# A feed-forward block product with seven half products in place of eight, its weight sums made on GpSimd

## The chip, the cores and the metric

One core of a Trainium2 chip. The metric is the device time of one execution in microseconds, the median of three runs.

## The reference, cut to what matters

Two layers, each a feed-forward half step, a mixer and a second feed-forward half step, on 256 tokens of width 1024, all in fp32:

```python
D_MODEL = 1024; SEQ = 256; DEPTH = 2; D_FF = 2816
def swiglu_ffn(h, w_up, w_down):
    gate, up = jnp.split(h @ w_up, 2, axis=-1)
    return (jax.nn.silu(gate) * up) @ w_down
...
    for l in range(DEPTH):
        x = x + 0.5 * swiglu_ffn(rms_norm(x, g_ffn1[l]), w_up1[l], w_down1[l])
        ...  # the mixer: recurrence and attention, not touched here
        x = x + 0.5 * swiglu_ffn(rms_norm(x, g_ffn2[l]), w_up2[l], w_down2[l])
```

## The kernel before

Every fp32 product is made of three products of rounded parts: an operand is split into a high part (rounded, type float32r) and a low part (what is left), and high x high, high x low and low x high are added in PSUM. The activations are split once per norm. The weights are split tile by tile as they stream in: a tile (`hc`, 512 KB: two blocks of 128 rows by 512 columns, or one by 1024) is loaded by SP into `raw` (`emit_dma`, five buffers), rounded by ACT into `whi` (`emit_hi`, L331, six buffers), and DVE subtracts to get `wlo` (`emit_lo`, L340, six buffers). TensorE then visits the tile once for each of the two token tiles of 128 (`visit`, L390): two blocks of rows, three matmuls each, so 6 matmuls a visit and 12 a tile. The high part of a tile can be made once the tile six places earlier has had both its visits.

A feed-forward (`ffn`, L603) goes through the hidden width in six chunks (`CH`: five of 512 columns, one of 256). For each chunk `block` makes gate for both token tiles (4 weight tiles), then up (4 tiles). ACT takes the gate out of PSUM through silu into `nat` (`ev_g`, L637), DVE multiplies with up (`ev_u`, L642), and a chain (`h_chain`) transposes that h: a copy into `tmp`, a transposing DMA issued by SP, a copy back by ACT or DVE (L318, L315), and a split into high and low parts (L502, L504). The down product of the chunk before follows each chunk but the first (`down`, 4 tiles).

The order on every engine is written out when the program is built: a planner (`Sched`) keeps a clock per engine, bills each instruction a cost, and lets chains of small work step in between matmuls when their time has come. `split` decides when the next `whi` and `wlo` are placed. The engines then run their queues strictly in this order and wait on semaphores.

POOL does little: constants at the start, the power for the norms (L551), powers for the attention's norms (L950), and its own DMA queue: 22 small loads of parameter rows (`load_rows`, L467 to L472) near the start, and four stores of a tensor of ones to DRAM (`ones_chain`, L681) that ACT prepares with copies (L677). Twelve large buffers (`slot`) hold activations, hidden chunks and scratch in turn.

## Time and profile before

| | us |
|---|---|
| median of 3 runs (1269.89 to 1270.96) | 1269.91 |
| the profiled execution, its own time | 1269.92 |
| its span in the profile | 1268.2 |
| TensorE busy | 1257.6 |
| DVE busy | 825.4 |
| ACT busy | 804.8 |
| POOL busy | 69.5 |

The time of a run and the span of its profile differ by 1.7 us, which lie outside the first and last instruction. Busy times of different engines overlap; a time is the sum of what ended last at each point, which for nearly all of this kernel is TensorE.

### The profile page before, as it was taken

The page shows a single profiled execution, that of the slowest core. Times are in us where ns is not written, and L with a number is a line of the kernel's source. Part 1 is how long each engine was busy: PE and PEld are TensorE (multiplying, and loading weights), DVE is VectorE, ACT ScalarE, POOL GpSimd, SP SyncE. Part 2 cuts the span into 40 slices and gives each one's busy share as a digit, 9 for nine tenths or more (in the row PEclk, how much of TensorE's full clock was granted, in tenths as well). Part 3 has the DMA queues.
Part 4 walks back from the last instruction along what each step waited for, and adds up shares of the span by engine and source line. Part 5 has one row for each costly group of instructions (what it writes and reads, how often), then busy time and mean ns, then how long its engine had stood idle before and what let it go on. Part 6 is the DMA issues. An engine that isn't in the chain of part 4 may idle for free.

```text
span 1268.2 us, 16349 instructions
## 1 busy us (share of the span) xinstructions
PE 1257.6 (99%) x5961; PEld 1039.6 (82%) x5961; DVE 825.4 (65%) x1164; ACT 804.8 (63%) x1076; POOL 69.5 (5%) x89
## 2 busy tenths in 40 slices
PE   9999999999999999999999999999999999999998
PEld 7888888888777888888888888888887878888887
DVE  6655558798676666555575545678977767655553
ACT  6657557886767556555566555679757764665553
POOL 4000000002200000000000000000042000000000
PEclk9999999999999999999999999999999999999999
DMA  7967769676444568676678777597764345687762
GB/s 258 264 207 225 217 172 277 161 218 202 148 141 150 168 198 217 209 208 207 179 220 217 213 216 216 158 249 190 210 206 149 126 150 182 193 222 216 216 199 76
DMA packets 193489, 248.80 MB, mean 196 GB/s; under 512 B 73672, under 2 KB 86144, under 8 KB 193408
## 3 DMA queue, kind: packets, MB, share of 16 engines
q1 hardware_dynamic: 191472, 244.49, 64.8%
q0 software_dynamic: 1920, 3.26, 1.0%
q8 instruction: 47, 0.77, 0.2%
q14 instruction: 34, 0.28, 0.1%
q10 hardware_dynamic: 16, 0.00, 0.0%
HBM read 229.88 MB, written 2.10 MB: 183 GB/s over the span
## 4 chain that ended last, share of the span: by engine, by line
PE 94%; DVE 3%; ACT 1%; DMA 1%; issue 1%; SPq 0%; POOL 0%; ACTq 0%; DVEq 0%
PE x L397 14%; PE x L399 13%; PE x L398 13%; PE z L398 12%; PE z L397 12%; PE z L399 12%; PE y L397 4%; PE y L399 4%; PE y L398 4%; PE z L481 2%; PE z L1008 1%; PE z L818 1%; DVE wlo L340 1%; PE y L1070 1%; DMA raw<-in_w_up_dram 1%
## 5 line engine op out<-in xcount | busy, mean ns | idle before, releaser
L340 DVE TENSOR_TENSOR wlo<-raw,whi 128x1024 fp32r<-128x1024 f32 x423 | 510.3, 1221 | 218.8 <-ACT whi L331 211.4
L331 ACT CAST whi<-raw 128x1024 fp32r<-128x1024 f32 x423 | 440.3, 1049 | 209.2 <-PE z L399 118.0
L397 PE MATMUL x<-whi,s 128*128 128x512 f32 x800 | 322.4, 403 | 4.8 <-DVE nat L954 2.8
L399 PE MATMUL x<-whi,s 128*128 128x512 f32 x800 | 312.5, 391 | 0.0
L398 PE MATMUL x<-wlo,s 128*128 128x512 f32 x800 | 312.2, 390 | 0.0
L398 PE MATMUL z<-wlo,s 128*128 128x512 f32 (+1 forms) x752 | 279.5, 372 | 0.1
L397 PE MATMUL z<-whi,s 128*128 128x512 f32 (+1 forms) x752 | 279.3, 371 | 0.0
L399 PE MATMUL z<-whi,s 128*128 128x512 f32 (+1 forms) x752 | 279.1, 371 | 0.0
L397 PEld LDWEIGHTS x<-whi,s 128*128 128x128 f32 x800 | 150.3, 188 | 38.8 <-issue 2.9
L399 PEld LDWEIGHTS x<-whi,s 128*128 128x128 f32 x800 | 150.2, 188 | 33.3 <-DVE s L504 0.9
L398 PEld LDWEIGHTS x<-wlo,s 128*128 128x128 f32 x800 | 150.5, 188 | 29.4 <-DVE wlo L340 0.6
L398 PEld LDWEIGHTS z<-wlo,s 128*128 128x128 f32 x752 | 141.7, 188 | 25.9 <-DVE wlo L340 1.8
L397 PEld LDWEIGHTS z<-whi,s 128*128 128x128 f32 x752 | 141.7, 188 | 24.4
L399 PEld LDWEIGHTS z<-whi,s 128*128 128x128 f32 x752 | 141.7, 188 | 24.4
L318 ACT COPY tmp<-nat 128x1024 uint16<-128x1024 uint16 (+1 forms) x88 | 96.3, 1114 | 76.2 <-DMA nat<-tmp 68.2
L397 PE MATMUL y<-whi,s 128*128 128x512 f32 x208 | 82.3, 396 | 0.0
L399 PE MATMUL y<-whi,s 128*128 128x512 f32 x208 | 81.1, 390 | 0.0
L398 PE MATMUL y<-wlo,s 128*128 128x512 f32 x208 | 81.0, 390 | 0.0
L642 DVE SCALAR_TENSOR_TENSOR nat<-z,rstd,nat 128x512 f32<-128x512 f32 (+1 forms) x48 | 33.9, 706 | 57.9 <-PE z L399 57.9
L504 DVE TENSOR_TENSOR s<-tmp,s 128x512 fp32r<-128x512 f32 (+1 forms) x71 | 46.6, 657 | 27.4 <-ACT s L502 26.9
L637 ACT ACTIVATE nat<-z,rstd 128x512 f32<-128x512 f32 (+1 forms) x46 | 30.0, 652 | 47.1 <-PE z L399 47.0
L502 ACT CAST s<-tmp 128x512 fp32r<-128x512 f32 (+1 forms) x71 | 42.0, 592 | 20.6 <-DVE tmp L531 19.8
(161 smaller groups left out, 891.0 us busy)
## 6 DMA issues: line engine op xcount, KB each, us to landing
raw<-in_w_up_dram SPq DMA_DIRECT2D x175, 512.0 KB, 4.6
raw<-in_w_in_dram SPq DMA_DIRECT2D x112, 512.0 KB, 4.4
raw<-in_w_down_dram SPq DMA_DIRECT2D x88, 512.0 KB, 4.4
raw<-in_w_lru_out_dram SPq DMA_DIRECT2D x16, 512.0 KB, 3.8
raw<-in_w_attn_out_dram SPq DMA_DIRECT2D x16, 512.0 KB, 3.8
raw<-in_w_o_dram SPq DMA_DIRECT2D x16, 512.0 KB, 4.3
s<-ones_d POOLq DMA_DIRECT2D x16, 128.0 KB, 4.4
tmp<-in_b_gate_dram SPq DMA_DIRECT2D x8, 256.0 KB, 4.3
```

The costliest lines, as they stand in the source:

```text
L318: nc.scalar.copy(out_, in_)
L331: nc.scalar.copy(hi, raws[i])
L340: nc.vector.tensor_tensor(out=lo, in0=raws.pop(i), in1=f32(hi), op=ALU.subtract)
L397: nc.tensor.matmul(acc, lhsT=lhs(0, k0 + kk)[:, ts], rhs=hi[:, kk, :], start=st, stop=False)
L398: nc.tensor.matmul(acc, lhsT=lhs(0, k0 + kk)[:, ts], rhs=lo[:, kk, :], start=False, stop=False)
L399: nc.tensor.matmul(acc, lhsT=lhs(1, k0 + kk)[:, ts], rhs=hi[:, kk, :], start=False, stop=sp)
L481: nc.tensor.transpose(dst_ps[:, j * P:(j + 1) * P], src[:, j * P:(j + 1) * P], ident)
L502: nc.scalar.copy(hi, t)
L504: nc.vector.tensor_tensor(out=lo, in0=t, in1=f32(hi), op=ALU.subtract)
L637: nc.scalar.activation(s[tok][0], acc, AF.Silu, scale=rs(tok))
L642: nc.vector.scalar_tensor_tensor(out=h, in0=acc, scalar=rs(tok), in1=h, op0=ALU.mult, op1=ALU.mult)
L818: nc.tensor.matmul(ps[:, g, :], lhsT=wax[0][:, g, n, :], rhs=xr[0][:, n, :], start=True, stop=True)
```

## The change

For chunks 2 and 4 of every feed-forward (`SEVEN`), gate and up are made as one product of 2 x 2 blocks. The activations are cut into two token tiles by two halves of the 1024 inputs, the weights into two halves of the inputs (rows 0 to 511 and 512 to 1023) by gate and up columns. With Winograd's form of Strassen's scheme seven products of half the depth give all four results, where the plain form needs eight. Four of the seven weight operands are sums: t3 = 22 - 12, t1 = 12 - 11, t2 = 11 + t3, t4 = 21 - t2, made by POOL in fp32 on the loaded tiles (`sums`, L279 of the new file), and then split into high and low parts as any tile. Four activation operands are sums too; POOL makes them once per feed-forward (`sums_chain`, L721 and L728), and ACT and DVE split them. Each of the seven products has two weight tiles, each visited once: 14 tiles of 6 matmuls in place of 8 tiles of 12. The results come together in four buffers of SBUF (`w`): ACT copies the first product, DVE adds the others out of PSUM with seven sums (L757), and the gating follows as before (L764, L769). The products run in the order 11, t1, t2, 21, t3, 22, t4.

The eight loads of a block go to five slots, in the order 11, 12, 22, 21, and are issued in a row right behind the load ahead of them. The loads of the parameter rows stay where they were in time, and their transposes come 45 us earlier, so that their slot comes free.

```diff
+GPS = 2.3
...
+SEVEN = (2, 4)
...
+    ORDER = ("11", "t1", "t2", "21", "t3", "22", "t4")
...
+        def load(self, name, u, src):
+            if not self.t:
+                for k in ("11", "12", "22", "21", "t3"):
+                    self.t[k] = slot([P, 4, 512])
+            nc.sync.dma_start(out=self.part(name, u), in_=src)
+            if name != "12":
+                raws[self.index(name, u)] = self.part(name, u), 0.0
+            if (name, u) == ("21", 1):
+                self.chain = S.add(self.sums(), S.now + 6.0, "g")
+        def sums(self):
+            def op(name, u, dst, a, b, f):
+                o = self.part(dst, u)
+                nc.gpsimd.tensor_tensor(out=o, in0=self.part(a, u), in1=self.part(b, u), op=f)
+                raws[self.index(name, u)] = o, S.use("g", GPS)
+            for u in range(2):
+                op("t3", u, "t3", "22", "12", ALU.subtract)
+                yield S.t["g"], "g"
+                op("t1", u, "12", "12", "11", ALU.subtract)
+                yield S.t["g"], "g"
+            for name, dst, a, b, f in (("t2", "11", "t3", "11", ALU.add), ("t4", "21", "21", "11", ALU.subtract)):
+                for u in range(2):
+                    while nxt["lo"] <= self.index(dst, u):
+                        yield S.now + 0.5, "g"
+                    op(name, u, dst, a, b, f)
+                    yield S.t["g"], "g"
...
+    def plan_seven(w, f0):
+        st = Seven()
+        sevens.append(st)
+        for name, r0, c0 in (("11", 0, f0), ("12", 0, FF + f0), ("22", 512, FF + f0), ("21", 512, f0)):
+            for u in range(2):
+                r = r0 + 256 * u
+                loads.append((w[r:r + 256, c0:c0 + 512].rearrange("(k p) n -> p k n", p=P), (st, name, u)))
+        for _ in range(14):
+            hcs.append((2, 512))
+            uses.append(1)
 
...
+        raws[i] = t, 0.0
+        while loads and isinstance(loads[0][1], tuple):
+            src, (st, name, u) = loads.pop(0)
+            st.load(name, u, src)
...
-        if can_hi() and nxt["hi"] - nxt["pos"] <= lead and (idle is None or S.busy("a") < idle):
+        if can_hi() and nxt["hi"] - nxt["pos"] <= lead and (
+                idle is None or S.busy("a") < idle) and raws[nxt["hi"]][1] <= max(S.now, S.t["a"]) + 0.05:
...
+        def sums_chain():
+            for tok in range(NT):
+                for hf in range(2):
+                    yield nrm.done[tok, hf]
+            xh, xl = nrm.xT[0][0], nrm.xT[1][0]
+            a, b = slot([P, KD, T]), slot([P, 4, 4, P])
+            for q in range(2):
+                yield S.t["g"], "g"
+                ks = slice(4 * q, 4 * q + 4)
+                nc.gpsimd.tensor_tensor(out=a[0][:, ks], in0=f32(xh[:, ks]), in1=f32(xl[:, ks]), op=ALU.add)
+                S.use("g", GPS)
+            A = lambda tok, q: a[0][:, 4 * q:4 * q + 4, tok * P:(tok + 1) * P]
+            B = lambda i: b[0][:, i]
+            for i, u, v, f in ((0, A(1, 0), A(1, 1), ALU.add), (1, B(0), A(0, 0), ALU.subtract),
+                               (2, A(0, 0), A(1, 0), ALU.subtract), (3, A(0, 1), B(1), ALU.subtract)):
+                yield S.t["g"], "g"
+                nc.gpsimd.tensor_tensor(out=B(i), in0=u, in1=v, op=f)
+                S.use("g", GPS / 2)
+            free(a)
+            sums[0], sums[1] = slot([P, 4, 4, P], F32R), slot([P, 4, 4, P], F32R)
+            yield S.t["g"], "a"
+            for q in range(2):
+                ii = slice(2 * q, 2 * q + 2)
+                yield from split_seg(b[0][:, ii], sums[0][0][:, ii], sums[1][0][:, ii], 1024)
+                yield S.now, "a"
+            free(b)
+        sums_c = S.add(sums_chain(), S.now + 4.0, "g", True)
...
+        def seven(c):
+            st = sevens.pop(0)
+            S.need(sums_c)
+            xh = lambda tok, q: lambda e, k: nrm.xT[e][0][:, 4 * q + k, tok * P:(tok + 1) * P]
+            xs = lambda i: lambda e, k: sums[e][0][:, i, k, :]
+            w = slot([P, 4, 512])
+            s1, u2, u4, c22 = (w[0][:, i] for i in range(4))
+            h, b5 = {}, []
+            def prod(name, lhs_, fin):
+                b, r = zbank()
+                for u in range(2):
+                    visit(st.index(name, u), b, lhs_, 2 * u, None, u == 0, u == 1, (lambda: fin(b, r)) if u else None)
+            def plus(dst, x, y, dep=0.0):
+                nc.vector.tensor_tensor(out=dst, in0=x, in1=y, op=ALU.add)
+                return S.use("d", dve_c(512), dep)
+            def gate(tok, src, dep):
+                nrm.scaled(tok)
+                h[tok] = new_nat()
+                S.func("silu")
+                nc.scalar.activation(h[tok][0], src, AF.Silu, scale=rs(tok))
+                return S.use("a", act_c(512, 1), dep)
+            def up(tok, src, dep):
+                t, rh = h[tok]
+                nc.vector.scalar_tensor_tensor(out=t, in0=src, scalar=rs(tok), in1=t, op0=ALU.mult, op1=ALU.mult)
+                dep = S.use("d", dve_c(512), dep)
+                hch[c, tok] = rh.user = S.add(h_chain(c, tok, t, rh, dep), dep)
+            def after_1(b, r):
+                nc.scalar.copy(s1, b)
+                S.use("a", act_c(512))
+                r.free = True
+            def after_6(b, r):
+                plus(u2, b, s1)
+                r.free = True
+                plus(u4, b5[0], u2)
+            def after_2(b, r):
+                end = plus(s1, b, s1)
+                r.free = True
+                gate(0, s1, end)
+            def after_7(b, r):
+                plus(u2, b, u2)
+                r.free = True
+                plus(c22, b5[0], u2)
+                b5[1].free = True
+            def after_3(b, r):
+                end = plus(u4, b, u4)
+                r.free = True
+                up(0, u4, end)
+            def after_4(b, r):
+                end = plus(u2, b, u2)
+                r.free = True
+                up(1, c22, gate(1, u2, end))
+            prod("11", xh(0, 0), after_1)
+            prod("t1", xs(0), lambda b, r: b5.extend((b, r)))
+            prod("t2", xs(1), after_6)
+            prod("21", xh(0, 1), after_2)
+            prod("t3", xs(2), after_7)
+            prod("22", xs(3), after_3)
+            prod("t4", xh(1, 1), after_4)
+            take(14)
...
-        yield S.now + 70.0, "p"
+        yield S.now + 25.0, "p"
```

What this does to the queues, at three places.

The first is the start of the program. POOL's queue before: the two powers of the first norm, then the loads of the parameter rows into `s0`.

```order
L551 TENSOR_TENSOR rstd_110<-msum_109,mhalf_99 128x1 x2
L467 DMA s0_1_101<-in_g_ffn1_dram 8x128
L467 DMA s0_1_101<-in_g_mix_dram 8x128
L467 DMA s0_1_101<-in_g_ffn2_dram 8x128
L467 DMA s0_1_101<-in_conv_b_dram 8x128
L467 DMA s0_1_101<-in_b_a_dram 8x128
```

And now (`s1` and `s2` are the high and low parts of the activations, `s4` their sum, `s5` the four sums of quarters):

```order
L631 TENSOR_TENSOR rstd_110<-msum_109,mhalf_99 128x1 x2
L721 TENSOR_TENSOR s4_36_277<-s1_9_149,s2_10_150 128x1024 x2
L728 TENSOR_TENSOR s5_37_278<-s4_36_277 128x512
L728 TENSOR_TENSOR s5_37_278<-s5_37_278,s4_36_277 128x512
L728 TENSOR_TENSOR s5_37_278<-s4_36_277 128x512
L547 DMA s0_1_101<-in_g_ffn1_dram 8x128
...
L551 DMA s0_1_101<-in_g_k_dram 1x16x4 x2
L552 DMA bfb_106<-in_b_forget_dram 128x16
L728 TENSOR_TENSOR s5_37_278<-s4_36_277,s5_37_278 128x512
```

Five sums stand between the powers and the 22 loads, and the sixth behind the loads. ACT's queue before, from the last roundings of chunk 0 into chunk 1 (`whi_60` and `whi_63` are tiles 10 and 11, the third and fourth of chunk 1's gate):

```order
L331 CAST whi_48_324<-raw_25_216 128x1024
L331 CAST whi_49_358<-raw_37_285 128x1024
L331 CAST whi_52_367<-raw_43_309 128x1024
L331 CAST whi_60_401<-raw_45_313 128x1024
L331 CAST whi_63_413<-raw_51_362 128x1024
L318 COPY tmp_66_422<-nat_40_300 128x1024
```

And now (`s6` takes the high parts of `s5`; `whi_64` is tile 10):

```order
L404 CAST whi_50_331<-raw_25_216 128x1024
L404 CAST whi_53_368<-raw_39_289 128x1024
L404 CAST whi_56_377<-raw_45_314 128x1024
L582 CAST s6_51_363<-s5_37_278 128x1024 x2
L404 CAST whi_64_414<-raw_47_319 128x1024
L404 CAST whi_67_426<-raw_55_372 128x1024
```

Two casts of `s5` stand ahead of tile 10; the second of them reads what POOL's sixth sum writes.

The second place is the ones, in the first feed-forward's chunk 1. ACT's queue before:

```order
L331 CAST whi_162_918<-raw_149_838 128x1024
L677 COPY s6_165_931<-ident_93 32x1024 x3
L502 CAST s5_119_690<-tmp_155_863 128x4x128
L677 COPY s6_165_931<-ident_93 32x1024
L677 COPY s7_166_942<-ident_93 32x1024 x4
L690 CAST fw_168_951<-tmp_167_949 128x8x16
L331 CAST whi_173_974<-raw_152_851 128x1024
```

And now, ACT and then POOL:

```order
L870 COPY s0_104_604<-ident_93 32x1024 x3
L404 CAST whi_105_611<-raw_79_476 128x1024
L870 COPY s0_104_604<-ident_93 32x1024
L870 COPY s0_106_616<-ident_93 32x1024 x4
L883 CAST fw_108_625<-tmp_107_623 128x8x16
L582 CAST s8_71_449<-tmp_109_627 128x4x128
L404 CAST whi_113_661<-raw_84_511 128x1024
```

```order
L728 TENSOR_TENSOR s5_37_278<-s4_36_277,s5_37_278 128x512
L279 TENSOR_TENSOR s5_89_517<-s11_87_515,s10_86_514 128x1024
L279 TENSOR_TENSOR s10_86_514<-s10_86_514,s9_85_513 128x1024
L279 TENSOR_TENSOR s5_89_517<-s11_87_515,s10_86_514 128x1024
L279 TENSOR_TENSOR s10_86_514<-s10_86_514,s9_85_513 128x1024
L874 DMA ones_d0_111<-s0_104_604 64x1024 x2
L874 DMA ones_d1_112<-s0_106_616 64x1024 x2
```

The copies go into one slot (`s0`) twice, where there were two slots, and the stores out of it stand behind four weight sums.

The third is a block in the middle, chunk 2 of the second layer's first feed-forward. DVE's queue before, in the down product of the chunk before and the gate that follows:

```order
L340 TENSOR_TENSOR wlo_1142_5928<-raw_1122_5830,whi_1137_5910 128x1024
L340 TENSOR_TENSOR wlo_1147_5964<-raw_1125_5838,whi_1146_5956 128x1024
L340 TENSOR_TENSOR wlo_1151_5978<-raw_1132_5880,whi_1149_5968 128x1024
L340 TENSOR_TENSOR wlo_1155_5992<-raw_1134_5888,whi_1150_5976 128x1024
L340 TENSOR_TENSOR wlo_1158_6006<-raw_1141_5922,whi_1154_5990 128x1024
L642 SCALAR_TENSOR_TENSOR nat_1144_5947<-z_1157_5996,rstd_110,nat_1144_5947 128x512
L315 COPY tmp_1162_6035<-nat_1144_5947 128x1024
```

And now, from the first tile of t2 (`s4`) to the fourth sum:

```order
L413 TENSOR_TENSOR wlo_1207_6092<-s4_1164_5877,whi_1201_6070 128x1024
L584 TENSOR_TENSOR s3_1152_5819<-tmp_1193_6016,s3_1152_5819 128x4x128
L413 TENSOR_TENSOR wlo_1208_6098<-s4_1164_5877,whi_1202_6079 128x1024
L413 TENSOR_TENSOR wlo_1211_6110<-s11_1167_5880,whi_1206_6090 128x1024
L413 TENSOR_TENSOR wlo_1213_6118<-s11_1167_5880,whi_1209_6104 128x1024
L413 TENSOR_TENSOR wlo_1215_6129<-s6_1168_5881,whi_1212_6116 128x1024
L413 TENSOR_TENSOR wlo_1218_6140<-s6_1168_5881,whi_1214_6127 128x1024
L757 TENSOR_TENSOR s8_1204_6082<-z_1216_6131,s8_1204_6082 128x512
L757 TENSOR_TENSOR s8_1204_6082<-z_1210_6106,s8_1204_6082 128x512
L413 TENSOR_TENSOR wlo_1222_6161<-s5_1166_5879,whi_1217_6138 128x1024
L413 TENSOR_TENSOR wlo_1223_6166<-s5_1166_5879,whi_1219_6150 128x1024
L757 TENSOR_TENSOR s8_1204_6082<-z_1220_6152,s8_1204_6082 128x512
```

Where a tile's split stood for 12 matmuls it now stands for 6, and the sums out of `z` stand between the splits.

## Rows read from the trace of the kernel before

**Rows 1.** The page: busy us, share of span, instructions; then the chain by engine.

```profile
PE 1257.6 (99%) x5961; PEld 1039.6 (82%) x5961; DVE 825.4 (65%) x1164; ACT 804.8 (63%) x1076; POOL 69.5 (5%) x89
PE 94%; DVE 3%; ACT 1%; DMA 1%; issue 1%; SPq 0%; POOL 0%; ACTq 0%; DVEq 0%
```

**Rows 2.** Windows view: us, PE, PEld, DVE, ACT, POOL busy (instructions), clock, DMA share, GB/s.

```profile
660.00:682.00 22.00, 22.00 (x99) 18.23 (x98) 13.26 (x14) 14.29 (x16) 0.00 (x0) 1.00 0.86 209
```

**Rows 3.** Timeline of PE: start, us, instruction; 24 matmuls lie between these two starts.

```profile
480.43 0.39 PE L397 MATMUL z<-whi,s 128*128 128x512 f32 x1
...
485.87 0.39 PE L397 MATMUL z<-whi,s 128*128 128x512 f32 x1
```

**Rows 4.** The page's groups (count, busy, mean ns), then DVE's timeline in the first 20 us.

```profile
L340 DVE TENSOR_TENSOR wlo<-raw,whi 128x1024 fp32r<-128x1024 f32 x423 | 510.3, 1221 | 218.8 <-ACT whi L331 211.4
L331 ACT CAST whi<-raw 128x1024 fp32r<-128x1024 f32 x423 | 440.3, 1049 | 209.2 <-PE z L399 118.0
13.76 1.28 DVE L531 TENSOR_TENSOR tmp<-z,g1col 128x512 f32<-128x512 f32 x2
17.29 3.50 DVE L340 TENSOR_TENSOR wlo<-raw,whi 128x1024 fp32r<-128x1024 f32 x3 [0.36 <-ACT whi L331]
```

**Rows 5.** Timeline of POOL from the start: all it does before 36 us, in part.

```profile
1.08 0.29 POOL masks.py:199 TENSOR_SCALAR_AFFINE_SELECT ident<-ident 128x128 f32<-128x128 f32 x1
...
1.83 0.31 POOL L1190 MEMSET posm<- 128x256 f32 x1
...
16.23 1.39 POOL L551 TENSOR_TENSOR rstd<-msum,mhalf 128x1 f32<-128x1 f32 x2 [13.06 <-DVE msum L549]
17.57 0.72 POOL L467 DMA_DIRECT2D s<-in_g_ffn_dram  x1
...
34.99 0.59 POOL L472 DMA_DIRECT2D bfb<-in_b_forget_dram  x1
```

**Rows 6.** Timelines of ACT and DVE from 28 to 33 us.

```profile
28.66 1.05 ACT L331 CAST whi<-raw 128x1024 fp32r<-128x1024 f32 x1 [2.24 <-PE z L399]
29.75 2.59 DVE L340 TENSOR_TENSOR wlo<-raw,whi 128x1024 fp32r<-128x1024 f32 x2 [1.03 <-ACT whi L331]
32.81 0.75 DVE L642 SCALAR_TENSOR_TENSOR nat<-z,rstd,nat 128x512 f32<-128x512 f32 x1 [0.48 <-PE z L399]
```

**Rows 7.** ACT, POOL and PE from 99 to 111 us; landing of the stores to ones_d.

```profile
99.05 3.15 ACT L677 COPY s<-ident 32x1024 f32<-32x1024 f32 x3
...
102.88 5.29 ACT L677 COPY s<-ident 32x1024 f32<-32x1024 f32 x5
102.50 0.56 POOL L681 DMA_DIRECT2D ones_d<-s  x1 [66.93 <-ACT s L677]
110.75 0.50 PE L398 MATMUL z<-wlo,s 128*128 128x512 f32 x1
DMA to landing us min/median/max: 2.9/2.9/3.0
```

**Rows 8.** ACT near 692 us; then DMA issues, 645 to 720 us.

```profile
692.17 1.35 ACT L318 COPY tmp<-nat 128x1024 uint16<-128x1024 uint16 x1 [2.98 <-DMA nat<-tmp]
raw<-in_w_up_dram SPq DMA_DIRECT2D x21, 512.0 KB, 4.7
nat<-tmp SPq DMA_TRANSPOSE x6, 4.5
```

**Rows 9.** POOL's powers of 128x8 and DVE's splits beside them, from 304 to 324 us.

```profile
304.86 2.59 POOL L950 TENSOR_TENSOR rq<-rq,mhalf 128x8 f32<-128x8 f32 x1 [4.38 <-DVE rq L948]
311.91 2.57 POOL L950 TENSOR_TENSOR rq<-rq,mhalf 128x8 f32<-128x8 f32 x1 [3.46 <-DVE rq L948]
322.17 1.64 POOL L950 TENSOR_TENSOR rq<-rq,mhalf 128x8 f32<-128x8 f32 x1 [2.60 <-DVE rq L948]
304.72 1.23 DVE L340 TENSOR_TENSOR wlo<-raw,whi 128x1024 fp32r<-128x1024 f32 x1
311.73 3.69 DVE L340 TENSOR_TENSOR wlo<-raw,whi 128x1024 fp32r<-128x1024 f32 x3
```

More of the change, by code (lines that the diff above doesn't have):

```diff
@@ L323, in can_hi @@
         i = nxt["hi"]
-        return i < NHC and i in raws and (i < RING or used[i - RING] == NT)
+        return i < NHC and i in raws and (i < RING or used[i - RING] == uses[i - RING])
     def emit_hi():
@@ L383, in get_hc @@
             if nxt["hi"] == nxt["lo"]:
+                for st in sevens:
+                    if st.i0 <= nxt["hi"] < st.i0 + 14:
+                        while nxt["hi"] not in raws:
+                            S.step(st.chain, True)
                 assert can_hi()
@@ L392, in visit @@
         hi, lo = get_hc(i)
-        _, nk, ncol = hcs[i]
-        ts = slice(tok * P, tok * P + P)
+        nk, ncol = hcs[i]
+        ts = slice(tok * P, tok * P + P) if tok is not None else slice(0, P)
         for kk in range(nk):
@@ L402, in visit @@
                 used[i] += 1
[L403 removed]
+                if used[i] == uses[i]:
                     ready.pop(i)
@@ new lines, in ffn @@
+        sums_c = S.add(sums_chain(), S.now + 4.0, "g", True)
[58 more added lines that the diff above has]
+            take(14)
+            st.release()
+            free(w)
+            if c == SEVEN[-1]:
+                free(sums[0])
+                free(sums[1])
```

60 lines of the change are left out of this document (41 added, 19 removed).

## The prediction

> **What bounds the kernel now.** I read the page's busy shares and its chain first. TensorE is busy 1257.6 of 1268.2 us and holds 94% of the chain; VectorE (DVE) and ScalarE (ACT) are busy about 65% each, GpSimd (POOL) 5% [rows 1]. So time can only come off by taking matmuls away, and only if DVE, ACT and POOL still keep ahead. Then I took one stretch in the middle of a feed-forward: in 22 us TensorE never pauses while DVE works 13.3 and ACT 14.3 [rows 2]. The slack of the two is real there, but it is 8 us in 22, and the change spends it in short stretches. One matmul of 512 columns costs the distance between starts: 24 of them lie between 480.43 and 485.87, so 0.2267 us each [rows 3] (the 0.39 of a record is a modelled length).
>
> The profiled run took 1269.9 us, which is the median of the runs; its span is 1268.2. I sum changes on 1269.9.
>
> **What goes.** Gate and up of a 512-wide chunk are 96 matmuls before and 84 after. Two chunks in each of four feed-forwards make 8 blocks: 8 x 12 x 0.2267 = 21.8 us less on the path. Nothing else leaves it.
>
> **What comes, per block.** Fourteen weight tiles in place of eight, each used for one token tile only, so a tile lasts TensorE 1.36 us instead of 2.72, while its two halves cost ACT 1.05 and DVE 1.22 as before [rows 4]. DVE gets seven extra sums of 512 columns out of PSUM, ACT one copy. POOL gets eight sums of two SBUF tensors of 128x1024. No row shows such a POOL instruction. The bounds: a memset of 256 columns takes 0.31 us, so four of them 1.24 (writes only); a select of 128 columns that reads one tensor takes 0.29, so eight of them 2.3; two reads could double that to 4.6 [rows 5]. I take 2.3, from the row that reads. The Trainium skill, GPSIMD Engine Reference, section 3.1, gives 4497 ns for a two-input sum of 2048 columns; half of that, an estimate of 2.25 us, would give 1342 us at the end.
>
> **Term A, the first feed-forward: +14.5.** The order shows the sums of the activations on POOL ahead of the 22 small loads of the parameter rows, and the last half sum behind them; on ACT the rounding of that last sum stands ahead of the rounding of the third gate tile of chunk 1. Before, POOL finished its powers at 17.6 and issued the 22 loads from 17.57 to 35.58, 18.0 us [rows 5]; nobody waited for that. After: 2 x 2.3 + 3 x 1.15 = 8.05 of sums, so the loads run from 25.7 to 43.7; the last half sum ends at 44.8, ACT's cast at 45.9, the tile's high part at 46.9, its low part at 48.1. Before, that tile's parts were made at 28.66 and 29.75 [rows 6]. TensorE wants it two tiles into chunk 1's gate: the gating product at 32.81 follows the last up product, so the gate starts at about 32.4 and the tile is due at 35.1. That is 13.0 us of TensorE standing. The next tile comes later by what DVE does between the two (a low part of sums 1.14, a gating product 0.67, the low part 1.14, against 1.36 of matmuls): 1.6 more. Bounds: 10.3 with sums at 1.24 us; 17 if the split of tiles on DVE also holds POOL up.
>
> **Term B, the first block: +8.5.** Eight copies on ACT prepare two tensors of ones that POOL sends to DRAM. Before, the tensors lay in two slots, the copies ran through at 99.05 and 102.88, and the first store was issued 0.3 us after its copies [rows 7]. Now the one free slot is used twice: the fifth copy waits for the first stores, and these stand on POOL behind four sums. From the start of the sums: 9.2 + 0.55 + 2.9 to land = 12.65; four copies fill 4.2 of it; ACT then stands 8.5 with the tiles' roundings behind it. There is no reserve: already before, a matmul slipped at 110.75, behind the copies [rows 7]. Bounds 4.2 (sums at 1.24) and 10.5 (sums start after the copies do).
>
> **Term C, every block: 8 x 9.2 = +73.** This is the uncertain one. In the printed DVE order, from the second product's first tile to the first tile of the down product that follows, DVE has 13 tile splits at 1.14 (three take 3.50), 7 sums and 2 splits of h at 0.60 (two take 1.28), one gating product of 0.75 [rows 4, 6]: 20.9 us. TensorE needs 6 x 12 x 0.2267 = 16.3 for the same stretch. The ring of six would let DVE start 9 us early, but ACT's copy of the transposed h stands ahead of these tiles; it waited 2.98 us for its transfer already before, with a transfer landing 4.5 after its issue [rows 8]. SP now puts eight 512 KB loads ahead of it in a row, and I leave 3.5 us of head start. So 20.9 - 16.3 - 3.5 = 1.1 us are missing in each block with POOL left out of it.
>
> With POOL it is more. When a DVE split was running, POOL's power of 128x8 took 2.59 and 2.57 us; with DVE out of SBUF it took 1.64, and in both slow cases it ended 1.5 us after the split did (305.95 to 307.45; 312.95 to 314.48), with two more splits queued in the second case [rows 9]. So POOL's two-tensor reads wait for a running DVE split, and get their turn between two of them. What no row shows is DVE waiting for POOL, since a power of eight columns reads for no time. The Trainium skill, SBUF: State Buffer, section "Who interferes with whom", says that a DVE instruction with two SBUF inputs contends with a GpSimd instruction that reads SBUF, and that the one that starts first holds the shared ports for its whole length; the rows agree for DVE first. By that rule all four late sums would hold DVE: 10.3 a block, 1353 us; if the wait went one way only, 1.1 a block.
>
> I take it that it goes both ways: each of POOL's last sums (two for the third product, two for the seventh, which wait for DVE's own splits) that falls into DVE's full stretch costs DVE its 2.3 us. Four fall there at most; the first may be over in time, so 3.5 x 2.3 = 8.05, and 9.2 a block. Bounds: 5.7 with two of them, 12 with sums of 2.6 and a late transfer.
>
> **Moved and free.** Loads keep their bytes. POOL's tiny powers come at the ends of feed-forwards, where its queue is empty. The parameter rows' transposes come 45 us earlier and still find their loads landed, since TensorE stands in A; without A they would wait for them. In the other three feed-forwards the six sums of activations (9.2 us of POOL) run beside chunks 0 and 1, with no loads behind them; the 8 us in 22 that DVE has free there hide them, and if not, two or three us each are lost.
>
> **Sum:** 1269.9 - 21.8 + 14.5 + 8.5 + 73 = 1344 us.
>
> **Rivals.**
> 1. *DVE is not held by POOL.* For it: no row shows DVE waiting. Against: POOL waits for DVE to the hundredth of a microsecond, so the path is shared, and a shared path that POOL streams through for 2.3 us should be closed to DVE. Then C is 0 to 1.5 a block: 1271 to 1283, about 1275. A and B alone still eat the gain.
> 2. *Faster: sums are cheap.* If a sum costs what a memset's slope says, 1.24 us, and DVE is not held, A is 10.3, B 4.2, C nothing: 1269.9 - 21.8 + 14.5 = 1262.6. It decides where A + B + 8C falls under 21.8, that is with sums below 2.1 us and C near nothing. Against: the instruction reads two tensors, and the nearest row that reads one already gives 2.3.
> 3. *Both ways and worse.* Sums slower than 2.3, or stretched by the splits: 12 a block, 1367; with sums of 3 us about 1385.
>
> **How the numbers follow.** My forecast, with rival 3 as its upper part, gets 0.72 and spans 1300 to 1390; rival 1 gets 0.17, rival 2 gets 0.11. A measurement tells about 0.2% (2.5 us) from no change: faster is below 1267.4, which is rival 2 and a little of rival 1, 0.12; the same is the low end of rival 1, 0.05; slower is 0.83. To leave out no more than 2 in 10 the range takes in rival 1 and stops short of rival 2 and of the far end above: 1266 to 1385. The forecast's own range is 1300 to 1385.
>
> **What would show it.** A: one pause of TensorE of 13 to 17 us near 35 us, ended by a tile whose rounding follows a POOL sum at about 45. B: one of 8 us or so in the first block, behind a copy that waits for a POOL store. C: in each block DVE splits that take or wait 2 us longer exactly while a POOL sum runs, and TensorE pausing before the third and fifth products for 3 to 4 us each. If DVE's splits keep their 1.22 us beside the sums, C is wrong and rival 1 holds; if POOL's sums last 1.2 us, rival 2; if the sums last 4 us, all three terms are too small. No row shows a clock under full speed, so what a pause of A's length does to TensorE's clock has no price here; it could only add.

## The result, and the profile after

The changed kernel takes 1362.74 us (median of 5 runs, 1361.15 to 1363.47), against 1269.91 (1269.25 to 1270.96) before: a ratio of 1.0724, interval 1.0712 to 1.0736. The forecast was slower, 1344, in a range of 1266 to 1385.

The page of the changed kernel: the engines (answers to [rows 1]), the chain by engine, then three groups of instructions (by line, engine, operation and tile: count, busy us, mean ns of one, and the idle time before them with what ended it).

```profile
PE 1268.9 (93%) x5865; PEld 1029.0 (76%) x5865; DVE 1039.5 (76%) x1272; ACT 860.0 (63%) x1144; POOL 317.4 (23%) x177
...
PE 65%; DVE 17%; DMA 8%; issue 5%; ACT 2%; POOL 2%; SPq 0%; DVEq 0%; ACTq 0%; POOLq 0%
...
L413 DVE TENSOR_TENSOR wlo<-raw,whi 128x1024 fp32r<-128x1024 f32 x359 | 453.9, 1291 | 81.3 <-ACT whi L404 79.5
...
L279 POOL TENSOR_TENSOR s<-s,s 128x1024 f32<-128x1024 f32 x64 | 192.0, 3019 | 317.3 <-DMA s<-in_w_up_dram 228.1
L413 DVE TENSOR_TENSOR wlo<-s,whi 128x1024 fp32r<-128x1024 f32 x112 | 211.7, 1929 | 29.4 <-ACT whi L404 29.4
```

TensorE held 94% of the chain before and holds 65% now; DVE came from 3% to 17%, the transfers (DMA) from 1% to 8%. The splits of tiles that lie in the slots (`wlo<-s`, the seven products' tiles) take 1929 ns each where a split took 1221 [rows 4], and POOL's 64 sums 3019 ns each.

TensorE's waits, in all (engine, line, whom it waited for; us in total, times, longest):

```profile
PE z L478 <- DVE wlo L413: 56.1, 39, 4.3
PE x L478 <- DVE wlo L413: 11.7, 10, 6.2
```

With two waits for high parts of 9.41 and 5.19 us, which stand below, that makes 82 us of waits for the parts of weight tiles. To place them I took the distance between the starts of successive 512-column matmuls, less the 0.2267 us of [rows 3], wherever it was over 0.26. Before, these losses are 20.5 us in all, after, 133.1; 133.1 - 20.5 - 21.8 = 90.8 of the 93.5 us between the spans (the rest lies in other shapes and missing records). They fall so:

| place | us lost after | foretold |
|---|---|---|
| waits from 22 to 30 us, beside the sums of activations | 4.0 (0.4 before) | none |
| the pause that ends at 49 us, and the slow matmuls behind it | 12.6 | A: 14.5 |
| first block: a pause that ends at 83 us | 7.3 | none |
| first block: a pause that ends at 91 us | 7.9 | B: 8.5 |
| the eight blocks, 6.4 to 11.2 each | 79.9 | C: 73 |
| all else | 21.4 (20.1 before) | |

**Place A.** POOL, then ACT, then TensorE around 40 us (start, us, instruction, count, idle time before it and what ended it); answers to [rows 5, 6]:

```profile
17.87 6.51 POOL L721 TENSOR_TENSOR s<-s,s 128x1024 f32<-128x1024 f32 x2
...
31.02 0.74 POOL L547 DMA_DIRECT2D s<-in_g_ffn_dram  x1
...
45.65 1.27 POOL L728 TENSOR_TENSOR s<-s,s 128x512 f32<-128x512 f32 x1
...
46.95 1.04 ACT L582 CAST s<-s 128x1024 fp32r<-128x1024 f32 x1 [17.03 <-POOL s L728]
47.90 1.99 ACT L404 CAST whi<-raw 128x1024 fp32r<-128x1024 f32 x2
...
48.99 0.80 PE L477 MATMUL z<-whi,s 128*128 128x512 f32 x1 [9.41 <-ACT whi L404]
```

The 22 loads start at 31.02, the last half sum follows at 45.65, its cast ends at 47.99, tile 10's rounding follows, and TensorE stands 9.41 us.

**The first block.** SP, DVE, ACT and TensorE there; answers to [rows 7, 8]:

```profile
71.22 7.48 SPq L597 DMA_TRANSPOSE nat<-tmp  x1
...
80.41 1.16 DVE L388 COPY tmp<-nat 128x1024 uint16<-128x1024 uint16 x1 [12.36 <-DMA nat<-tmp]
...
85.03 4.21 ACT L870 COPY s<-ident 32x1024 f32<-32x1024 f32 x4 [12.98 <-DMA ones_d<-s]
...
83.39 0.80 PE L478 MATMUL x<-wlo,s 128*128 128x512 f32 x1 [6.21 <-DVE wlo L413]
...
91.08 0.80 PE L477 MATMUL x<-whi,s 128*128 128x512 f32 x1 [5.19 <-ACT whi L404]
```

Two pauses, not one. For the first DVE stands 12.36 us for the transposed h, whose transfer SP issues from 71.22 on (7.48 us in its queue), behind the eight loads and three of the down product; the tile's split stands behind that copy. For the second, ACT's fifth copy waits 12.98 us for the stores of the ones.

**A block in the middle.** POOL, DVE, ACT and TensorE in chunk 2 of the last feed-forward:

```profile
1205.97 17.68 POOL L279 TENSOR_TENSOR s<-s,s 128x1024 f32<-128x1024 f32 x6 [24.57 <-DMA s<-in_w_up_dram]
1228.87 6.60 POOL L279 TENSOR_TENSOR s<-s,s 128x1024 f32<-128x1024 f32 x2 [5.22 <-DVE wlo L413]
...
1206.47 6.32 DVE L413 TENSOR_TENSOR wlo<-s,whi 128x1024 fp32r<-128x1024 f32 x2
...
1218.54 2.90 DVE L584 TENSOR_TENSOR s<-tmp,s 128x512 fp32r<-128x512 f32 x1
1221.36 4.50 DVE L413 TENSOR_TENSOR wlo<-s,whi 128x1024 fp32r<-128x1024 f32 x2
...
1226.39 10.16 DVE L413 TENSOR_TENSOR wlo<-s,whi 128x1024 fp32r<-128x1024 f32 x5
...
1223.68 1.99 ACT L404 CAST whi<-s 128x1024 fp32r<-128x1024 f32 x2 [1.20 <-POOL s L279]
...
1224.79 0.79 PE L478 MATMUL z<-wlo,s 128*128 128x512 f32 x1 [3.84 <-DVE wlo L413]
```

POOL's first six sums (t3's and t1's four, then t2's two) take 17.68 us, 2.95 each. Beside them the two DVE splits of the weight block 11 take 6.32, a split of h 2.90 (the next one, at 1225.79, 0.68), and the two splits from 1221.36 on 4.50: the first of these, of t1's second tile, is over only at 1224.73, behind t2's last sum, which ends at 1223.65. TensorE's pause of 3.84 us ends with it, so it lies inside the second product, between t1's two tiles. The cast at 1223.68, of t2's second tile, had been waiting for that same sum, but no wait of TensorE ends with it. The five splits from 1226.39 on are t2's second tile, 21's two and t3's two; beside the last two sums (t4's) they take 10.16 and not 5.76, as they do in the runs without sums below.

### The profile page after: what moved, and what is told of

Read it like the earlier page. It is cut to its first block, busy times and chain, and to the rows that moved or that the text cites. A ratio compares the mean times of both kernels' runs of the same rounds, so it can differ in the third digit from the quotient of the medians.

```text
span 1361.7 us, 16517 instructions
## 1 busy us (share of the span) xinstructions
PE 1268.9 (93%) x5865; PEld 1029.0 (76%) x5865; DVE 1039.5 (76%) x1272; ACT 860.0 (63%) x1144; POOL 317.4 (23%) x177
## 3 DMA queue, kind: packets, MB, share of 16 engines
q0 software_dynamic: 1920, 3.26, 0.9%
## 4 chain that ended last, share of the span: by engine, by line
PE 65%; DVE 17%; DMA 8%; issue 5%; ACT 2%; POOL 2%; SPq 0%; DVEq 0%; ACTq 0%; POOLq 0%
DVE wlo L413 12%; PE x L478 11%; PE x L477 11%; PE x L479 11%; PE z L478 6%; PE z L477 6%; PE z L479 6%; DMA nat<-tmp 6%; PE y L477 2%; PE y L479 2%; PE y L478 2%; DVE s L584 2%; PE z L561 2%; DVE s L757 1%; PE z L1201 1%
## 5 line engine op out<-in xcount | busy, mean ns | idle before, releaser
L413 DVE TENSOR_TENSOR wlo<-raw,whi 128x1024 fp32r<-128x1024 f32 x359 | 453.9, 1291 | 81.3 <-ACT whi L404 79.5
L404 ACT CAST whi<-raw 128x1024 fp32r<-128x1024 f32 x359 | 367.7, 1047 | 130.9 <-PE x L479 54.7
L477 PE MATMUL z<-whi,s 128*128 128x512 f32 (+1 forms) x720 | 272.2, 378 | 9.4 <-ACT whi L404 9.4
L479 PE MATMUL z<-whi,s 128*128 128x512 f32 (+1 forms) x720 | 272.4, 378 | 0.0
L279 POOL TENSOR_TENSOR s<-s,s 128x1024 f32<-128x1024 f32 x64 | 192.0, 3019 | 317.3 <-DMA s<-in_w_up_dram 228.1
L413 DVE TENSOR_TENSOR wlo<-s,whi 128x1024 fp32r<-128x1024 f32 x112 | 211.7, 1929 | 29.4 <-ACT whi L404 29.4
L477 PEld LDWEIGHTS z<-whi,s 128*128 128x128 f32 x720 | 139.1, 193 | 34.8 <-ACT whi L404 9.8
L479 PEld LDWEIGHTS z<-whi,s 128*128 128x128 f32 x720 | 139.3, 193 | 22.3
L391 ACT COPY tmp<-nat 128x1024 uint16<-128x1024 uint16 (+1 forms) x92 | 100.7, 1096 | 69.3 <-DMA nat<-tmp 64.5
L404 ACT CAST whi<-s 128x1024 fp32r<-128x1024 f32 x112 | 114.3, 1048 | 32.5 <-POOL s L279 19.8
L631 POOL TENSOR_TENSOR rstd<-msum,mhalf 128x1 f32<-128x1 f32 x12 | 8.2, 683 | 406.7 <-DVE msum L629 406.7
L584 DVE TENSOR_TENSOR s<-tmp,s 128x512 fp32r<-128x512 f32 (+1 forms) x71 | 63.6, 896 | 40.0 <-ACT s L582 39.6
```

What stands on the lines that cost most here:

```text
L279: nc.gpsimd.tensor_tensor(out=o, in0=self.part(a, u), in1=self.part(b, u), op=f)
L391: nc.scalar.copy(out_, in_)
L404: nc.scalar.copy(hi, raws[i][0])
L413: nc.vector.tensor_tensor(out=lo, in0=raws.pop(i)[0], in1=f32(hi), op=ALU.subtract)
L477: nc.tensor.matmul(acc, lhsT=lhs(0, k0 + kk)[:, ts], rhs=hi[:, kk, :], start=st, stop=False)
L479: nc.tensor.matmul(acc, lhsT=lhs(1, k0 + kk)[:, ts], rhs=hi[:, kk, :], start=False, stop=sp)
```

## The experiments

All but one are edits of the changed kernel. Times are medians, with the range of the runs behind them.

### The row loads behind the sums

```diff
     def rows_chain():
-        yield 20.0, "p"
+        yield 30.0, "p"
...
-        yield S.now + 25.0, "p"
+        yield S.now + 20.0, "p"
```

> The 22 loads of the parameter rows are issued after all six sums of the activations; nothing else is meant to move. If term A is the place of the last half sum behind the loads, TensorE's pause of 9.4 us at 49 us and the slow matmuls behind it (9.6 + 3.1 us lost) go, and about 12.5 us come off 1362.7: 1350, with 2 or 3 us of early waits beside POOL's sums left before 32 us. The rival, that the third gate tile is late anyway because DVE and ACT are behind after the sums, leaves a pause of 5 us or more and 1356 or more.

Measured: 1347.45 (1347.17 to 1349.06), 15.3 us less. The sixth sum now starts at 31.14, ahead of the loads, and no pause is left between 31 and 75 us. The waits before 31 us stay at 4.3. So the place of one half sum behind 22 loads is the pause; of the 2.7 us above the 12.6, 1.7 come from the first block, whose losses went from 21.6 to 19.9. POOL's timeline in this run, the sixth sum:

```profile
31.14 2.27 POOL L728 TENSOR_TENSOR s<-s,s 128x512 f32<-128x512 f32 x1
```

### One slot for both tensors of ones, no reuse

```diff
-        for hf in range(2):
-            t = slot([P, 2, KD // 2, T])
+        t = slot([P, 2, KD // 2, T])
+        for hf in range(2):
...
-                    nc.scalar.copy(t[0][one, e], bc(...))
+                    nc.scalar.copy(t[0][one, e ^ hf], bc(...))
...
-                nc.gpsimd.dma_start(out=ones_d[hf][b, e], in_=t[0][b, e])
-            free(t)
+                nc.gpsimd.dma_start(out=ones_d[hf][b, e], in_=t[0][b, e ^ hf])
+        free(t)
```

> The second tensor of ones goes into the other halves of the one slot, which the first leaves empty, so the fifth copy waits for no store. Two pauses lie at the first block: 7.3 us at 83 us and 7.9 us (5.6 and slow matmuls) at 91 us. If the second is the fifth copy's wait (term B as predicted), about 7.9 us come off: 1355. The first should stay, since a copy on DVE waits 12.4 us there for a transposed h whose transfer stands behind eight loads. If both pauses hang on the ones, 15 us come off: 1347.5.

Measured: 1355.67 (1354.63 to 1356.07), 7.1 less. ACT's five copies run through (5.30 us) and the pause at 91 us is gone; the one at 84 us stays (5.72 us, for a split). B is the second pause alone. ACT's and TensorE's timelines in this run:

```profile
71.93 5.30 ACT L870 COPY s<-ident 32x1024 f32<-32x1024 f32 x5
...
83.87 0.79 PE L478 MATMUL x<-wlo,s 128*128 128x512 f32 x1 [5.72 <-DVE wlo L413]
```

### The sums taken away, and a POOL that is busy without reading

```diff
-                nc.gpsimd.tensor_tensor(out=o, in0=self.part(a, u), in1=self.part(b, u), op=f)
-                raws[self.index(name, u)] = o, S.use("g", GPS)
+                nc.gpsimd.tensor_tensor(out=o[:, :, :1], in0=self.part(a, u)[:, :, :1], in1=self.part(b, u)[:, :, :1], op=f)
+                raws[self.index(name, u)] = self.part("22", u) if name == "t3" else o, S.use("g", GPS)
```

> The weight sums on POOL work on two columns and not on 1024, in the same order on every engine, and t3's tiles are split from the loaded 22 (so gate and up are not the reference's). This takes away the sums' time and the time for which they could hold DVE. Prediction's term C (POOL's sums hold DVE): of about 10 us lost in each block some 1.1 are left, and of the first block's second pause (behind the four sums) nearly nothing: 1362.7 - 8 x 8.9 - 7 = 1285. Rival: the pauses come from the transposed h behind eight loads and from loads that land late, not from POOL; then 4 us or more are left in each block and the time is 1310 or more.

And, with the sum of two columns kept, the memsets in the place of the sum:

```diff
+                for _ in range(2):
+                    nc.gpsimd.memset(o, 1.0)
```

> Each weight sum is a sum of two columns and two memsets of the whole result (gate and up are not the reference's), in the same order on every engine: POOL is busy about as long (four memsets of 256 columns took 1.24 us, so two of 1024 about 2.5), but reads next to nothing of SBUF. If DVE is held because both read SBUF (the prediction's reason for C), DVE's splits keep 1.22 us beside the memsets, and only the lateness of the results is left, 1 to 4 us a block: 1285 to 1315. If what counts is that the results come late, and not that DVE is held, the blocks lose what they lose now, about 10 us each: 1355 or more. If any POOL instruction holds DVE, the splits last as long as beside the sums.

Measured: 1297.91 (1295.85 to 1299.29) without the sums, 64.8 less than the changed kernel; 1302.32 (1300.71 to 1305.42) with memsets. The order on each engine is the same in all three. Without the sums it is 13 us above what was expected: a block still loses about 2 us and not 1.1, and the place of the two pauses ahead of the first block 11.6 (15.3 before) and not 8. The rival asked for 1310 or more; it fell, though ACT still waits for the transposed h as long as before (66.1 us in all, 64.5 in the changed kernel). The page's group of splits out of the slots, without the sums:

```profile
L413 DVE TENSOR_TENSOR wlo<-s,whi 128x1024 fp32r<-128x1024 f32 x112 | 132.7, 1219 | 64.7 <-ACT whi L404 64.4
```

And with memsets:

```profile
L415 DVE TENSOR_TENSOR wlo<-s,whi 128x1024 fp32r<-128x1024 f32 x112 | 132.6, 1219 | 69.1 <-ACT whi L406 69.0
```

1219 ns in both, 1929 in the changed kernel: 112 x 0.71 = 79.5 us of DVE were spent standing. In the same block, by POOL's and DVE's timelines with memsets, POOL fills where it summed, in the middle of the five DVE splits, and these take 5.76:

```profile
1183.44 1.97 POOL L281 MEMSET s<- 128x1024 f32 x2
...
1179.83 5.76 DVE L415 TENSOR_TENSOR wlo<-s,whi 128x1024 fp32r<-128x1024 f32 x5
```

A POOL that is nearly as busy (two memsets of 1024 are 1.97 us) but doesn't read costs 4.4 us in the whole program; one that reads costs 64.8. So it is the reading that costs, not that POOL is busy or that its results come late by the time it takes by itself.

### The pairs by themselves

No part of the kernel, but a program of its own, in sections that begin together:

```python
sub(6); meet()              # splits of 128x1024 on DVE alone
add(4); meet()              # sums of 128x1024 on POOL alone
sub(10); add(4); meet()     # both
sub(10); fill(8); meet()    # splits beside POOL memsets
plus(12); add(4); meet()    # DVE sums of 512 columns, one input in PSUM, beside POOL sums
copy(10); add(4); meet()    # DVE copies, SBUF to SBUF, beside POOL sums
cast(10); add(4); meet()    # ACT casts beside POOL sums
```

> Not the kernel but its pairs of instructions by themselves (the output is only a copy of x): six splits on DVE alone, four sums on POOL alone, then ten splits beside four sums, ten splits beside eight memsets, twelve DVE sums of 512 columns with one input in PSUM beside four POOL sums, ten DVE copies beside four sums, ten ACT casts beside four sums. If one port serves DVE's second input and POOL, splits and sums take turns: alone 1.15 and 2.4 us each, together the four sums and the first splits add up to their sum (4 x (2.4 + 1.15) = 14 us for four of each, DVE's ten splits last 11.5 + 9.6 = 21 us), and beside memsets, copies, PSUM sums and casts nobody is slower. Rival: both only slow each other by some tenths (bandwidth), in all pairs alike.

The timelines of DVE and POOL in it, by sections (the last row is POOL beside ACT's casts); each section's first DVE line (L208) adds two SBUF columns of one element:

```profile
6.25 6.90 DVE L213 TENSOR_TENSOR lo<-raw,hi 128x1024 fp32r<-128x1024 f32 x6
...
6.18 0.16 DVE L208 TENSOR_TENSOR m<-m,raw 128x1 f32<-128x1 f32 x1 [0.31 <-POOL m L207]
...
13.44 9.23 POOL L229 TENSOR_TENSOR po<-pa,pb 128x1024 f32<-128x1024 f32 x4
...
13.52 2.27 DVE L208 TENSOR_TENSOR m<-m,raw 128x1 f32<-128x1 f32 x1 [0.30 <-POOL m L207]
...
25.04 17.86 DVE L213 TENSOR_TENSOR lo<-raw,hi 128x1024 fp32r<-128x1024 f32 x10
...
22.77 12.24 POOL L229 TENSOR_TENSOR po<-pa,pb 128x1024 f32<-128x1024 f32 x4
...
43.36 11.44 DVE L213 TENSOR_TENSOR lo<-raw,hi 128x1024 fp32r<-128x1024 f32 x10
...
57.36 7.25 DVE L217 TENSOR_TENSOR sv<-z,sv 128x512 f32<-128x512 f32 x12
...
55.09 9.26 POOL L229 TENSOR_TENSOR po<-pa,pb 128x1024 f32<-128x1024 f32 x4
...
80.00 9.27 POOL L229 TENSOR_TENSOR po<-pa,pb 128x1024 f32<-128x1024 f32 x4
```

Alone a split takes 1.15 (6.90 / 6) and a sum 2.31 (9.23 / 4). Together ten splits take 17.86, 6.4 more than beside memsets (11.44), and four sums 12.24, 3.0 more: they take turns (the first sum holds the single-element instruction, the other three fall between splits, 2.1 us for each). The single-element DVE instruction took 0.16 by itself and 2.27 beside a running sum: DVE stands for the whole of a sum that it finds under way. DVE's sums out of PSUM (7.25 / 12 = 0.60, near the 0.64 of [rows 4]) aren't touched, and neither is POOL beside them (9.26) or beside ACT's casts (9.27). Beside DVE's copies the sums took longer (10.64 for four), against what was expected; what a copy takes alone was not measured, so that pair is left open.

### The loads spread

```diff
+        at = len(loads) - 3
         for name, r0, c0 in (("11", 0, f0), ("12", 0, FF + f0), ("22", 512, FF + f0), ("21", 512, f0)):
             for u in range(2):
                 r = r0 + 256 * u
-                loads.append((w[r:r + 256, c0:c0 + 512].rearrange("(k p) n -> p k n", p=P), (st, name, u)))
+                loads.insert(at + u, (w[r:r + 256, c0:c0 + 512].rearrange("(k p) n -> p k n", p=P), (st, name, u)))
+            at += 3
...
```

> The edits of the two runs before (row loads after the sums, one slot for the ones), and a block's eight loads in pairs behind each of the four loads ahead, not in a row behind the last. The two edits alone should give 1347.5 - 7.1 = 1340. If the transposed h waits behind the eight loads, the pause of 7 us at the first block goes, and ACT's wait of 7 us for it in each block; the loads also land 8 us earlier, so that about two more of POOL's sums are over before DVE's full stretch: 1340 - 5 - 8 x 4 = 1303. Rival: POOL's sums hold DVE as long wherever they fall, DVE has no room earlier either, and it stays above 1325.

Measured: 1344.78 (1344.14 to 1345.62). Its base, the two edits alone, was run later: 1343.04. So nothing is gained; the rival holds. The sums start earlier, and hold DVE there; the page's group for the splits out of `raw`:

```profile
L415 DVE TENSOR_TENSOR wlo<-raw,whi 128x1024 fp32r<-128x1024 f32 x359 | 479.6, 1363 | 66.9 <-ACT whi L406 65.7
```

Against the run with the two edits alone the splits out of `raw` went from 1294 to 1363 ns; those out of the slots went from 1864 to 1743.

### The sums on DVE

```diff
-                self.chain = S.add(self.sums(), S.now + 6.0, "g")
+                self.chain = S.add(self.sums(), S.now + 8.0, "d", True)
...
-                nc.gpsimd.tensor_tensor(out=o, in0=self.part(a, u), in1=self.part(b, u), op=f)
-                raws[self.index(name, u)] = o, S.use("g", GPS)
+                nc.vector.tensor_tensor(out=o, in0=self.part(a, u), in1=self.part(b, u), op=f)
+                raws[self.index(name, u)] = o, S.use("d", dve_c(1024))
...
```

> The edits of the first two runs, and the weight sums made by DVE and not by POOL, loads in a row as in the changed kernel. If POOL's sums hold DVE for their whole length, giving DVE the sums themselves costs it less (1.15 us a sum and not 2.4 to 3), and with POOL out of the way splits keep 1.22: of eight sums about four fall in the full stretch, 4.6 us a block in place of 10: 1340 - 8 x 4.5 = 1304. Rival: DVE has no room for any of the eight, 9.2 us a block on top of the 2 left without sums: 1350.

> Both edits of the two runs beside it together: loads spread and sums on DVE. If both reasons hold, the four early sums fall where DVE has 8 of 22 us free and only the four late ones cost, less the head start that the earlier transposes give: 1 to 4 us a block: 1275 to 1300. A kernel faster than before (1270) would need the sums to cost under 1 us a block.

Measured: 1336.38 (1334.99 to 1338.38), and with the loads spread 1332.24 (1330.04 to 1334.61). Faster than with POOL's sums by 6.7 us, and with the loads spread by 12.5, but far above both forecasts, which had put only the four late sums on the path. The splits are whole again, and a sum on DVE takes half of POOL's time. The page's groups with loads in a row:

```profile
L414 DVE TENSOR_TENSOR wlo<-s,whi 128x1024 fp32r<-128x1024 f32 x112 | 133.1, 1218 | 2.4 <-ACT whi L405 2.4
...
L279 DVE TENSOR_TENSOR s<-s,s 128x1024 f32<-128x1024 f32 x64 | 78.1, 1223 | 34.8 <-DMA s<-in_w_up_dram 33.6
```

There is no long pause in the later blocks; each loses 5.6 to 7.7 us in seven or so short waits of 0.4 to 1.3 us. DVE is simply full there, whichever engine makes the sums: in the block of chunk 2 in the last feed-forward it works 25.29 of the 25.5 us from 1200.0 on.

### What the sums cost, and which

Four kernels with the row loads behind the sums and one slot for the ones. In the second all sums are of two columns, by the edit shown above; in the last two those that the list in `c` names are (in the second and third, t3's tiles are read from the loaded 22):

```diff
+                c = (slice(None), slice(None), slice(0, 1 if name in (...) else 512))
-                nc.gpsimd.tensor_tensor(out=o, in0=self.part(a, u), in1=self.part(b, u), op=f)
+                nc.gpsimd.tensor_tensor(out=o[c], in0=self.part(a, u)[c], in1=self.part(b, u)[c], op=f)
```

> The row loads after the sums and one slot for both tensors of ones, together; the loads in a row and the weight sums on POOL as in the changed kernel. If terms A and B are separate pauses, the two gains add: 1362.7 - 15.3 - 7.1 = 1340. If they overlap (the later ones ended beside the second pause), 1345 or more. This is also what the three runs beside it are compared with.

> The two edits, and weight sums of two columns (gate and up are not the reference's): what is left of the change when the sums cost nothing. In the run with such sums alone, 1298, the pause at 49 us lost 13 us and the first block's 11.6: without them 1298 - 13 - 11 = 1274, with about 2 us a block and the sums of activations left. Below 1267 the change could win with cheaper sums; at 1270 or more it could not, whatever makes the sums.

> The two edits; of the eight sums of a block the first four (t3, t1) are of two columns, the last four (t2, t4) whole (gate and up are not the reference's). The prediction put the whole loss on the last four, which fall into DVE's full stretch (3.5 x 2.3 us = 8 a block): then this stays near the run with all eight, 1334 to 1340. Rival: DVE has no room ahead of the block either and every sum costs alike, 1 us each: 1340 - 32 = 1308.

> The two edits; of the eight sums of a block the first four (t3, t1) are whole, the last four (t2, t4) of two columns (gate and up are not the reference's). By the prediction the first four are hidden: near the run without sums, 1274 to 1282. Rival, every sum costs alike: 1308. If the first four come late (their loads land 10 us after they are issued) and delay the second product, 1300 or more with one long pause a block, and not many short ones.

| weight sums | us | above no sums |
|---|---|---|
| all eight | 1343.04 (1342.08 to 1344.14) | 61.6 |
| none | 1281.49 (1279.53 to 1282.96) | |
| t2 and t4 (late) | 1316.20 (1315.75 to 1319.45) | 34.7 |
| t3 and t1 (early) | 1282.98 (1282.50 to 1283.22) | 1.5 |

The two edits together took 19.7 us off the changed kernel, where each by itself had taken 15.3 and 7.1: A and B are separate but for 2.7 us. With the late sums alone the time lies between the forecast (1334 to 1340) and its rival (1308).

The timelines of POOL and DVE in the same block: POOL's whole sums, and DVE's five splits from t2's second tile to t3's second. With all eight sums:

```profile
1186.56 17.69 POOL L279 TENSOR_TENSOR s<-s,s 128x1024 f32<-128x1024 f32 x6 [25.09 <-DMA s<-in_w_up_dram]
1209.48 6.62 POOL L279 TENSOR_TENSOR s<-s,s 128x1024 f32<-128x1024 f32 x2 [5.22 <-DVE wlo L413]
...
1207.00 10.19 DVE L413 TENSOR_TENSOR wlo<-s,whi 128x1024 fp32r<-128x1024 f32 x5
```

With none:

```profile
1156.46 5.76 DVE L413 TENSOR_TENSOR wlo<-s,whi 128x1024 fp32r<-128x1024 f32 x5
```

With the late four:

```profile
1168.67 4.74 POOL L280 TENSOR_TENSOR s<-s,s 128x1024 f32<-128x1024 f32 x2
1184.85 6.59 POOL L280 TENSOR_TENSOR s<-s,s 128x1024 f32<-128x1024 f32 x2 [11.44 <-DVE wlo L414]
...
1182.36 10.15 DVE L414 TENSOR_TENSOR wlo<-s,whi 128x1024 fp32r<-128x1024 f32 x5
```

With the early four:

```profile
1158.08 5.76 DVE L414 TENSOR_TENSOR wlo<-s,whi 128x1024 fp32r<-128x1024 f32 x5
```

Early sums alone are hidden, to 0.2 us a block. Late sums alone cost 4.3 us a block, and the five splits say why: 10.15 and not 5.76, two sums (t4's) at 2.2 each; t2's two are over long before (POOL then idles 11.44 us). With all eight, t2's sums stand on POOL behind the early four: six in a row take 17.69, and only 5.22 us are left before t4's. The two of t2 then run while DVE makes a split of h and the split of t1's second tile, which the second product needs. By DVE's timeline these two take 2.88 and 3.36 us, where 0.68 and 1.22 are usual, and TensorE pauses 4.36 us before t1's second tile, with slow matmuls behind it. With the late four alone it doesn't. So the other 25 us, 3.2 a block, come from both halves together: the early sums push t2's to where they hold DVE. That t2's results are late costs nothing in this block, since both their roundings were over (1202.67, 1205.34) when DVE came to their splits (1205.26, 1207.00); memsets, late by their own time only, cost 0.6 a block.

With no weight sums at all (the sums of activations stay) the kernel is still 11 us slower than before (1281.49 to 1270.33 in that set of runs), so, in this order of the work, no cheaper way to make the weight sums would have made the change faster. I ran no version that beats the kernel before.

## Why the prediction was right, and where it was off

*Direction and place.* Slower, by three terms that each have their pause. The sum was 96 us of losses, and 111.3 were found (4.0 - 0.4 + 12.6, 7.3 + 7.9, 79.9); with 3.4 us in small places, and in what the distances of matmuls don't catch, this is the 18.7 us between 1344 and 1362.7.

*What goes.* 21.8 us by count of matmuls (5961 and 5865 on the two pages, 96 fewer); nothing in the runs speaks against it, and no run showed it alone.

*Term A, 14.5; measured 12.6 in the pause, 15.3 by the run that undoes it.* Right in its mechanism. The steps were off in both directions: a sum of 1024 columns took 3.26 beside DVE's splits and not 2.3, a half sum 2.15 to 2.26 and not 1.15, so the loads began at 31.0, not 25.7; but they took 14.6 us and not 18.0. That the two errors partly cancel is luck. The cast, the rounding and the pause follow as written. The case named beside the upper bound, splits and sums that hold each other up, is what happened, though not with its 17 us: seven splits from 17.58 took 15.71 us, 2.24 each. TensorE's waits for these splits, 3.6 us ahead of the pause, stood in no term, and they stay in the run that undoes A. DVE's timeline of the changed kernel:

```profile
17.58 15.71 DVE L413 TENSOR_TENSOR wlo<-raw,whi 128x1024 fp32r<-128x1024 f32 x7 [0.36 <-ACT whi L404]
```

*Term B, 8.5; measured 7.1.* Right in its mechanism. Beside it the step "SP now puts eight 512 KB loads ahead of it in a row" was charged with some lost head start in each block, and not with a pause of its own: 7.3 us in the first block. That term was missing. With the two edits alone the first block has two pauses of 3.2 and 3.1 us in its place, and with the loads spread three (3.2, 3.1 and 2.5), so it isn't shown that the order of transfers alone makes it.

*Term C, 73; measured 79.9.* The mechanism and the size came out; where the loss falls did not. That POOL's reading holds DVE is shown three ways: by the memsets (they cost 4.4 us where the sums cost 64.8), by the pairs, and by the five splits. By the Trainium skill, SBUF — State Buffer, section "Who interferes with whom", the first holder keeps the shared ports for its whole instruction and a GpSimd instruction that only writes doesn't contend with DVE's second input; the pairs agree in both (2.27 us for one element; 11.44 us for ten splits beside memsets). So rival 1 fell. The step "3.5 x 2.3 = 8.05" a block came near: in seven of the eight blocks of the changed kernel the four late sums hold DVE for about 8.7 us (2.2 each: a split of h, one of t1, and t3's two), and the weight sums together cost 61.6 / 8 = 7.7 a block. But it lacks a condition. Alone, the late sums cost 4.3 a block: t4's two hold DVE where it counts even so, t2's two only behind four early sums, which were billed at nothing. The early sums cost no DVE time that is missed where they stand (1.5 us in the program); they push t2's sums to where it is, and in that row a sum lasts 2.95 and not 2.3, since POOL is held too. And the part without POOL was put at 1.1 a block; with no weight sums a block loses about 2, waiting for splits in its last tiles, among the seven DVE sums out of PSUM.

*The price of a sum, 2.3.* Measured 2.31 alone. The Trainium skill, GPSIMD Engine Reference, section 3.1, gives 4497 ns for 2048 columns; half of it, an estimate, is 2.25. The two agree.

*Rivals.* Rival 2 (a sum at 1.24, no hold) fell on both counts. Rival 3 put the time at 1367 by 12 us a block; the time came near it by another way, C at 10 and a pause that nobody had listed. *What would show it:* A's pause was said to be 13 to 17 us and was 9.41, with 3.1 more behind it. Of the two pauses of 3 to 4 us in a block, said to stand before the third and the fifth product, one is there (3.84), but inside the second product, before t1's second tile; in the fifth, t3's second tile waits 1.67, and three tiles behind it 0.6 to 0.8.

## What to carry to other kernels

An idle engine whose instructions the busy one has to take turns with is not free capacity: price such an instruction as if the busy engine made it, and longer (64 sums of 2.31 us, 148 us of an idle POOL, cost 64.8 us of time). Before giving it a loop's work, see which of its instructions fall where the first engine has no slack, and what stands behind them in its own queue: 25 of the sums' 62 us came only with four sums that by themselves were hidden. And a saving of TensorE's time of 21.8 us, spread over eight short stretches, needs the splits of those stretches to fit: without any weight sums a block still lost about 2 us, and the whole change 11.
